# Part of the experts through DRAM, and a new order of the first loads, in a two-layer hybrid decoder

## Chip, cores and metric

The kernel runs on one core of one Trainium2 chip. The metric is the device time of one execution in microseconds (us); lower is better. Shown runs of the kernel before: 1222.70, 1228.84 and 1231.54 us.

## The reference

Two layers, each a mixer and a mixture of experts, over 512 tokens of width 1024, in float32. Both halves are preceded by RMSNorm and modulated by adaLN (shift, scale and gate, from `c_act @ w_ada[l] + b_ada[l]`).

```python
for l in range(DEPTH):
    shift_m, scale_m, gate_m, shift_f, scale_f, gate_f = split(c_act @ w_ada[l] + b_ada[l])
    h = rms_norm(x, norm_mix[l]) * (1 + scale_m) + shift_m
    x = x + gate_m * hybrid_mixer(h, w_in[l], ...)       # stick-breaking + gated linear attention
    h = rms_norm(x, norm_ffn[l]) * (1 + scale_f) + shift_f
    x = x + gate_f * hierarchical_moe(h, ...)
```

The mixture picks one of 4 groups for each token, then 2 of the group's 8 experts, and adds `(silu(h @ w_gate[e]) * (h @ w_up[e])) @ w_down[e]` with the two weights. An expert has 256 hidden units, so its three matrices have 1 MiB each; all 32 experts of a layer are read.

## The kernel before, in words

**Mixer.** `mixer` projects x to all heads in steps of 128 rows of `w_in`: `project` makes a load, a `prep` (split of the weights into a high and a low part) and a `run` of each step, and a list of steps sets their order. In layer 0 the adaLN vectors that the first projection needs are made on the way: `ada` loads 2 tiles of `w_ada`, multiplies them by c (the product `ada`), copies the result (`row`, L245) and turns it into columns (`adaT`). Eight such generators stand in `first`, two for each pair of steps, and all share one PSUM bank. The loads of the first two are issued before anything of `w_in` (L312). `transposed` (L361) runs them to their end before it modulates x. Twelve products of the identity (`warm`) run on TensorE (PE) ahead of that.

**Experts.** `moe` numbers 64 slots for each expert, 2048 in all, and goes over 16 pairs of experts, 128 slots each. The token rows of a pair are fetched from a DRAM copy `xg` by an indirect DMA on GpSimd's queue (`fetch`), transposed (`g`) and modulated (`gT`). Then

- `hidden`: 32 products `gu` with gate and up weights, silu, product: `hs`;
- `turn`: transposition of `hs` (`hsT`) and a copy on ScalarE (`hT`);
- `down`: 16 products `d` with the down weights; DVE scales them by routing weight and gate (`o`), ScalarE and GpSimd split `o` into `ohi` and `olo`;
- `places` and `combine`: a 0/1 matrix `oT` of slots against tokens, and 16 products `y` of `oT` with `ohi` and `olo` that spread the slots' rows to the 512 tokens; DVE adds them to x, one add of 128x512 for each of 8 units.

In the loop over pairs i, PE gets d of pair i-1, gu of pair i, then y of pair i-1 in four parts with transposes of later rows between them, and hsT after the third part.

**What sets the order of the loads.** SP (the sync engine) issues all weights in the order of `queue`: `(0, e)` is gate and up of expert e (5 buffers), `(1, e)` is down (4 buffers). The loop `for i in range(0, NE, 2)` at its head lists them as buffers come free: d of a pair frees two down buffers, gu of a pair two gate and up buffers. An issue waits for its buffer, and all behind it wait too. GpSimd's DMAs have a queue of their own; both run on the same 16 DMA engines.

**What the steps of the prediction touch.** `load_weights` and `queue`, `down`, `places`, the loop over i (from L1247), the head of `mixer` (L306 to L341) and `project`'s `load` and `prep` (L397 to L414).

Of the kernel before, what the change touches and what calls it, by code (L numbers as in the profile page):

```python
# [9 lines left out]
F = mybir.dt.float32  # L10
# [10 lines left out]
P = 128  # L21
# [3 lines left out]
NE, FE, CAP = 32, 256, 64  # L25
NX = 16


@with_exitstack
def hybrid_decoder_kernel(ctx, tc, x, c, w_ada, b_ada, norm_mix, norm_ffn, w_in, w_gk2, b_gk, q_gain,  # L30
# [181 lines left out]
    xs = dram.tile([S, D], F, name="xs")  # L212
    xg = dram.tile([S, D], F, name="xg")

    mod = [const.tile([P, 6, KT], F, name=f"mod{l}") for l in range(L)]
# [4 lines left out]
    bgk = cols[:, 96:100]  # L220


    def ada(l, c0, n, raw, bank, at, later=True):
# [12 lines left out]
        if later and vec in (2, 5) and not half:  # L236
            gates[l, vec] = (gts if vec == 5 else gms[l])([P, D])
            kept_dma(G, gates[l, vec], along(b_ada, l * 6 * D + vec * D, D))
        yield
        row = rowt[at]([P, n], name="row")  # L240

        ps = bank("ada")
        for k in range(KT):
            product(ps[32 * (k % 4):32 * (k % 4) + 32, 0:n], ct1[:, k:k + 1].to_broadcast([P, 32]), ws[k], k < 4, k >= 4)
        A.copy(row, ps[:, 0:n])  # L245
        yield
        if vec in (2, 5):
# [35 lines left out]
    def mixer(l, xt, ss, x_src, pool, later):  # L283
# [21 lines left out]
        if l == 0:  # L305
# [4 lines left out]
            for tt in range(NT):  # L310
                kept_dma(SY, xt[tt // 2][:, tt % 2], x_src[P * tt:P * tt + P, :])
            for g in first[0]:  # L312
                next(g)
        wv = w_in[l].rearrange("(k p) n -> p k n", p=P)
# [3 lines left out]
        for i, g in enumerate((q_gain, k_gain)):  # L318
            for h in range(2):
                G.dma_start(gain[64 * h:64 * h + 64, i:i + 1], g[l].rearrange("(d o) -> d o", o=1))  # L320
        V.tensor_scalar(gain[:, 1:2], gain[:, 1:2], 8.0, None, op0=OP.mult)
        glag = const.tile([P, P], F, name="glag", tag="glag")
# [17 lines left out]
        if l == 0:  # L340
            pm(ps[0:1, 0:1], ss[:, 0, 2:3], ident[:, 0:1], True, True)  # L341
        for _ in range(16 if l else 12):
            pm(ps[:, 0:P], ident, ident, True, True)
# [50 lines left out]
        def project(cols, n, nb, finish, feature=False, lead=False):  # L394
# [3 lines left out]
            def load(k):  # L398
                if k % 2 == 0:
# [5 lines left out]
                    for start, w in cols:  # L405
                        SY.dma_start(t[:, :, at:at + w], wv[:, k:k + 2, start:start + w])
                        at += w
                    held[k], held[k + 1] = t[:, 0], t[:, 1]

            def prep(k):  # L410
                if lead:
                    transposed(k)
                parts[k] = [whl([P, n], R, name="whl") for _ in range(2)]
                split(held.pop(k), *parts[k])  # L414

# [24 lines left out]
        def sb_qk(g):  # L440
            def finish(banks):
                qk = sbq[g] = xq([P, NT, 8, 64], name="qk")
                so = tiny.tile([P, NT, 8], F, name="sqk")
# [419 lines left out]
    def moe(l, xt, ss, pool):  # L863
# [10 lines left out]
        queue = [(0, 0), (0, 1), (0, 2), (0, 3), (0, 4), (1, 0), (1, 1), (1, 2), (1, 3)]  # L874
        for i in range(0, NE, 2):
            queue += [(0, e) for e in (i + 5, i + 6) if e < NE] + [(1, e) for e in (i + 4, i + 5) if e < NE]
        loaded = {}
# [12 lines left out]
        def load_weights(n):  # L890
            for _ in range(min(n, len(queue))):
                w, e = queue.pop(0)
                loaded[w, e] = load_expert(w, lambda src: src[l, e // 8, e % 8])

# [148 lines left out]
        def down(hT, ws, i=None):  # L1043
# [7 lines left out]
            for q in range(2):  # L1051
                pd = bank("d", "dy", 4)
                for j in range(2):
                    for e in range(n):
                        pm(pd[64 * e:64 * e + 64], hT[:, j, 64 * e:64 * e + 64],
                           ws[e][:, D * j + 512 * q:D * j + 512 * q + 512], j == 0, j == 1)
                o = ot([P, 512], name="o")
                gate = gates[l, 5][r, 512 * q:512 * q + 512]
# [3 lines left out]
                else:  # L1062
                    V.scalar_tensor_tensor(o, pd, cws[:, i:i + 1], gate, op0=OP.mult, op1=OP.mult)  # L1063
                    if last is not None:
# [18 lines left out]
        def places(i):  # L1083

            o1 = s2([P, S], name="o1")
            V.tensor_scalar(o1, slots_row[:, 0], sid[:, i:i + 1], None, op0=OP.is_equal)
            oT = (rows_ if i == NE // 2 - 1 else ohs)([P, S], R, name="oT")
            V.scalar_tensor_tensor(oT, slots_row[:, 1], sid[:, i:i + 1], o1, op0=OP.is_equal, op1=OP.add)
            return oT
# [11 lines left out]
        def combine_last(pairs):  # L1101
# [18 lines left out]
            for n, u in ((0, 5), (0, 6), (1, 0), (1, 1), (0, 7), (1, 2), (1, 3), (1, 4), (1, 5), (1, 6), (1, 7)):  # L1120
                unit(n, u)

        def spread(slot, slot0):
# [77 lines left out]
        keep_warm(lo.rearrange("p t e -> p (t e)"), 20)  # L1201
        fetched = [fetch(idx[:, i:i + 1]) for i in range(4)]


        with tc.issue_after(listed.ins), tc.issue_after(normed.ins):
# [15 lines left out]
            V.tensor_tensor(cw[:, :, 1:2], e2, gw, op=OP.mult)  # L1221
            dump(f"cw{l}", cw)
            exw = tmp.rearrange("p t k e -> p (t k) e")
            V.tensor_tensor(exw, ex.rearrange("p t k e -> p (t k) e"), cw.rearrange("p t k -> p (t k)")[:, :, None].to_broadcast([P, NT * 2, NE]), op=OP.mult)
# [20 lines left out]
        gT1, second = gather(fetched[1:2])  # L1245
        hs = None
        for i in range(NE // 2):  # L1247
            while not {(0, 2 * i), (0, 2 * i + 1)} <= set(loaded):
                load_weights(1)
            if i % 2 == 0:  # L1250
                now = gT
                if i < NE // 2 - 2:
                    gT, rest = gather(fetched[i + 2:i + 4])
                    fetched += [fetch(idx[:, j:j + 1]) for j in range(i + 4, min(i + 6, NE // 2))]
# [10 lines left out]
            if i == 0:  # L1265
                for _ in second:
                    pass
                weights_by_slot()
            for u in range(4):
                for v in range(2):  # L1270
                    if i:
                        combine(2 * u + v, *part)
                next(rest, None)
                if u == 2:
                    hT = turn(hs)
        last = []
        end = combine_last([part, last])
# [94 lines left out]
```

## Time and profile before

| | us |
|---|---|
| median of the three runs | 1228.84 |
| lowest, highest | 1222.70, 1231.54 |
| profiled execution | 1228.59 |
| its span, first to last instruction | 1226.4 |
| PE busy in the span | 1174.6 (96%) |
| DVE, ScalarE, GpSimd busy | 686.3, 473.6, 196.7 |
| granted TensorE clock, mean | 0.988 |

The profiled execution is one run; its span leaves out what lies before the first and after the last instruction. A group of rows below names its view. In the chain of waits, each row has a start, a length and what held the end back. In the windows, each row has a stretch and the busy time of each engine in it, the granted clock, the DMA engines' busy share and GB/s. In the rows of one tile, "DMA to landing" is the time from issue to landing of the loads in that window. Matmuls overlap, so a row of PE can be longer than the distance to the next.

### The profile page before, as it was taken

What the parts mean: (1) busy time and instruction counts of PE and PEld (TensorE: products, weight loads), DVE (VectorE), ACT (ScalarE), POOL (GpSimd) and SP (SyncE); (2) the same over time, 40 slices, a digit from 0 to 9 for tenths busy, and PEclk for the clock granted to TensorE, in tenths of its full rate; (3) what the DMA queues carried; (4) which work ended last, traced back from release to release, by engine and by line L of the source; (5) the groups of instructions that cost most, each with busy time, mean ns of one, the idle gap of its engine ahead of it and who ended that gap; (6) DMA issues with size and microseconds to landing.
All of it is one profiled execution on the core that took longest, in us unless ns stands there. A gap on an engine that the chain in (4) does not pass through costs nothing.

```text
span 1226.4 us, 17270 instructions
## 1 busy us (share of the span) xinstructions
PE 1174.6 (96%) x6467; PEld 749.3 (61%) x6467; DVE 686.3 (56%) x1336; ACT 473.6 (39%) x942; POOL 196.7 (16%) x231
## 2 busy tenths in 40 slices
PE   4999999999989999999999997999999899999997
PEld 3787867666765444444478775666876744444443
DVE  3474546465854555555566562545856565555553
ACT  4376656453243111111155764554624411111121
POOL 3000010011312222221110001001210222222110
PEclk8999999999999999999999999999999999999999
DMA  9652765643687999999445355563229599999981
GB/s 297 225 170 88 223 167 148 207 142 101 249 369 263 411 410 417 419 418 419 191 156 173 98 168 121 172 172 121 69 103 372 210 400 420 418 420 419 419 349 69
DMA packets 105926, 312.27 MB, mean 255 GB/s; under 512 B 12876, under 2 KB 49936, under 8 KB 81264
## 3 DMA queue, kind: packets, MB, share of 16 engines
q1 hardware_dynamic: 96720, 289.57, 63.4%
q0 software_dynamic: 9120, 21.57, 5.2%
q8 instruction: 52, 0.85, 0.3%
q14 instruction: 34, 0.28, 0.1%
HBM read 311.08 MB, written 8.40 MB: 260 GB/s over the span
## 4 chain that ended last, share of the span: by engine, by line
PE 85%; DMA 6%; DVE 5%; ACT 2%; issue 1%; SPq 1%; DVEq 0%; ACTq 0%
PE proj L74 19%; PE gu L78 18%; PE y L78 10%; PE d L78 9%; PE op L74 6%; PE z L74 5%; DMA wada<-in_w_ada_dram 3%; PE ada L78 3%; PE g L1003 2%; DMA raw<-in_w_in_dram 2%; PE warm L78 1%; PE pv L74 1%; PE lgT L74 1%; PE o L74 1%; PE adaT L78 1%
## 5 line engine op out<-in xcount | busy, mean ns | idle before, releaser
L78 PE MATMUL gu<-wgu,gT 128*64 128x512 f32 x1024 | 225.4, 592 | 0.1
L74 PE MATMUL proj<-whl,hh 128*128 128x512 f32 (+2 forms) x768 | 218.6, 368 | 0.1
L78 PEld LDWEIGHTS gu<-wgu,gT 128*64 128x64 f32 x1024 | 75.5, 137 | 143.7 <-issue 142.2
L74 PEld LDWEIGHTS proj<-whl,hh 128*128 128x128 f32 x768 | 133.5, 189 | 32.0 <-issue 10.0
L1076 DVE TENSOR_TENSOR x<-y,x 128x512 f32<-128x512 f32 x240 | 148.5, 683 | 0.9 <-PE y L78 0.9
L74 PE MATMUL proj<-whl,hl 128*128 128x512 f32 (+2 forms) x384 | 138.4, 362 | 0.0
L1031 DVE TENSOR_TENSOR hs<-hs,gu 128x256 f32<-128x256 f32 x32 | 13.5, 421 | 198.2 <-ACT hs L1030 198.2
L1069 POOL TENSOR_TENSOR olo<-o,ohi 128x512 fp32r<-128x512 f32 x60 | 76.9, 1283 | 263.5 <-ACT ohi L1068 263.3
L96 DVE TENSOR_TENSOR whl<-raw,whl 128x512 fp32r<-128x512 f32 (+2 forms) x128 | 72.7, 570 | 81.8 <-ACT whl L95 70.5
L78 PE MATMUL d<-wd,hT 128*64 128x512 f32 x512 | 116.9, 598 | 1.4 <-ACT hT L1040 1.4
L78 PE MATMUL y<-ohi,oT 128*128 128x512 f32 x240 | 104.5, 436 | 0.0
L95 ACT ACTIVATE whl<-raw 128x512 fp32r<-128x512 f32 (+2 forms) x128 | 66.6, 524 | 85.1 <-PE proj L74 66.9
L78 PE MATMUL y<-olo,oT 128*128 128x512 f32 x240 | 94.2, 393 | 0.0
L74 PEld LDWEIGHTS proj<-whl,hl 128*128 128x128 f32 x384 | 72.2, 188 | 14.3 <-issue 4.2
L1030 ACT ACTIVATE hs<-gu 128x256 f32<-128x256 f32 x32 | 12.3, 385 | 168.4 <-PE gu L78 168.4
L78 PEld LDWEIGHTS d<-wd,hT 128*64 128x64 f32 x512 | 33.9, 136 | 62.2 <-issue 48.1
L78 PEld LDWEIGHTS y<-ohi,oT 128*128 128x128 f32 x240 | 45.4, 189 | 31.8 <-issue 26.0
L1009 ACT ACTIVATE gT<-g,mod 128x256 f32<-128x256 f32 (+1 forms) x72 | 38.9, 544 | 61.6 <-DVE gT L1011 61.5
L1068 ACT ACTIVATE ohi<-o 128x512 fp32r<-128x512 f32 x60 | 37.8, 630 | 61.6 <-DVE o L1063 61.6
L1063 DVE SCALAR_TENSOR_TENSOR o<-d,cws,gate_f 128x512 f32<-128x512 f32 x64 | 47.8, 750 | 22.7 <-PE d L78 22.7
L736 POOL TENSOR_TENSOR raw<-raw,gate_m 128x1024 f32<-128x1024 f32 x16 | 40.2, 2520 | 122.6 <-DMA raw<-in_w_out_dram 68.2
L78 PE MATMUL ada<-wada,ct 128*32 128x512 f32 x320 | 49.1, 600 | 5.3 <-DMA wada<-in_w_ada_dram 5.3
(346 smaller groups left out, 1951.9 us busy)
## 6 DMA issues: line engine op xcount, KB each, us to landing
wgu<-in_w_gate_dram SPq DMA_DIRECT2D x64, 1024.0 KB, 9.5
wgu<-in_w_up_dram SPq DMA_DIRECT2D x64, 1024.0 KB, 11.7
wd<-in_w_down_dram SPq DMA_DIRECT2D x64, 1024.0 KB, 11.0
wada<-in_w_ada_dram SPq DMA_DIRECT2D x96, 512.0 KB, 5.1
raw<-in_w_in_dram SPq DMA_DIRECT2D x80, 256.0 KB, 4.4
raw<-in_w_out_dram SPq DMA_DIRECT2D x16, 512.0 KB, 4.1
raw<-in_w_in_dram SPq DMA_DIRECT2D x32, 128.0 KB, 4.2
xg<-xn POOLq DMA_DIRECT2D x8, 512.0 KB, 4.9
```

Of the source, the lines that this page charges most:

```text
L74: T.matmul(o, a, b, start=start, stop=stop, skip_group_check=True)
L78: tc.keep_in_program_order(T.matmul(o, a, b, start=start, stop=stop, skip_group_check=True))
L95: A.activation(hi, src, AF.Copy)
L96: eng.tensor_tensor(lo, src, hi.bitcast(F), op=OP.subtract)
L736: G.tensor_tensor(t, t, gates[l, 2][:, None, cols].to_broadcast([P, 2, 512]), op=OP.mult)
L1003: tc.keep_in_program_order(T.transpose(ps[:, at:at + P], r[:, P * k:P * k + P], ident))
L1009: A.activation(o, src, AF.Identity, scale=m, bias=b)
L1031: V.tensor_tensor(hs[r], hs[r], gu[r, 256:512], op=OP.mult)
L1063: V.scalar_tensor_tensor(o, pd, cws[:, i:i + 1], gate, op0=OP.mult, op1=OP.mult)
L1068: A.activation(hi, o, AF.Copy)
L1069: (G if last is None else V).tensor_tensor(lo, o, hi.bitcast(F), op=OP.subtract)
L1076: V.tensor_tensor(xc, ps, xc, op=OP.add)
```

## The change

**Experts.** The pairs are taken in the order of the table `ORDER`, which puts the first four (experts 0 to 7, all of group 0) at positions 1, 4, 7 and 10. For these four, `down` writes the scaled `o` (two tiles of 128x512) to a DRAM tensor `ys` by DMAs on GpSimd's queue; there is no split, no `places` and no `combine`. After the fourth, `take_back` fetches for each of 4 token tiles and 2 choices the 128 rows of `ys` at the tokens' slots (slots past the first 512 are left out by the bounds check), and DVE adds them to x under a mask `ysm`. Six of the eight are issued in steps 12 to 14, two behind the loop. In the step behind a spread pair, `down` comes after `hidden`, and `queue` is listed to match.

**Start.** The first two adaLN generators issue their loads behind those of the first `w_in` tile; the split of that tile's first half stands behind the copy of the adaLN row; `gain` is scaled later; 8 warm-up products in place of 12 in layer 0.

```diff
+NY = 4
+ORDER = [4, 0, 5, 6, 1, 7, 8, 2, 9, 10, 3, 11, 12, 13, 14, 15]
...
-        A.copy(row, ps[:, 0:n])
+        copied.append(A.copy(row, ps[:, 0:n]))
...
-            for g in first[0]:
-                next(g)
...
-        V.tensor_scalar(gain[:, 1:2], gain[:, 1:2], 8.0, None, op0=OP.mult)
...
-        for _ in range(16 if l else 12):
+        for _ in range(16 if l else 8):
...
                     held[k], held[k + 1] = t[:, 0], t[:, 1]
+                    if lead and k == 0:
+                        for g in first.get(0, ()):
+                            next(g)
...
-                split(held.pop(k), *parts[k])
+                if lead and k == 0 and l == 0:
+                    with tc.issue_after(copied[-1].ins):
+                        split(held.pop(k), *parts[k])
+                else:
+                    split(held.pop(k), *parts[k])
...
-        for i in range(0, NE, 2):
-            queue += [(0, e) for e in (i + 5, i + 6) if e < NE] + [(1, e) for e in (i + 4, i + 5) if e < NE]
+
+        freed = [(0, 0)]
+        for i in range(1, NE // 2):
+            freed += [(0, i), (1, i - 1)] if ORDER[i - 1] < NY else [(1, i - 1), (0, i)]
+        for w, i in freed:
+            queue += [(w, e) for e in ((2 * i + 4, 2 * i + 5) if w else (2 * i + 5, 2 * i + 6)) if e < NE]
...
-                o = ot([P, 512], name="o")
+                m = NY if i is None else ORDER[i]
+                o = (ohl if m < NY else ot)([P, 512], name="o")
...
-                    V.scalar_tensor_tensor(o, pd, cws[:, i:i + 1], gate, op0=OP.mult, op1=OP.mult)
+                    V.scalar_tensor_tensor(o, pd, cws[:, m:m + 1], gate, op0=OP.mult, op1=OP.mult)
+                    if m < NY:
+                        kept_dma(G, ys[P * m:P * m + P, 512 * q:512 * q + 512], o)
+                        continue
...
+        def take_back(tt, k):
+
+            r = rows_([P, D], name="back")
+            G.indirect_dma_start(r, None, ys[:, :], bass.IndirectOffsetOnAxis(ap=ysi[:, tt, k:k + 1], axis=0),
+                                 bounds_check=NY * P - 1, oob_is_err=False)
+            xc = xt[tt // 2][:, tt % 2]
+            return lambda: V.scalar_tensor_tensor(xc, r, ysm[:, tt, k:k + 1], xc, op0=OP.mult, op1=OP.add)
...
-            if i:
+            by_dram = i > 0 and ORDER[i - 1] < NY
+            if i and not by_dram:
                 part = places(i - 1), down(hT, [loaded.pop((1, e)) for e in (2 * i - 2, 2 * i - 1)], i - 1)
             *_, hs = hidden(gT1 if i == 1 else now, 0 if i < 2 else P * (i % 2), [loaded.pop((0, e)) for e in (2 * i, 2 * i + 1)])
+            if by_dram:
+                down(hT, [loaded.pop((1, e)) for e in (2 * i - 2, 2 * i - 1)], i - 1)
             load_weights(4)
...
+            if by_dram:
+                for _ in range(4):
+                    next(rest, None)
+                hT = turn(hs)
+                continue
             for u in range(4):
                 for v in range(2):
                     if i:
                         combine(2 * u + v, *part)
+                if i >= NE // 2 - 4 and u % 2 == 0:
+                    taken.append(take_back(*back.pop(0)))
+                    if len(taken) > 1:
+                        taken.pop(0)()
                 next(rest, None)
```

How the order changes, at three places. First SP's list of loads in layer 0's expert stage, behind the nine loads ahead; before, gate and up of two experts and two down loads take turns:

```order
L887 DMA wgu<-in_w_gate_dram 128x2048
L887 DMA wgu<-in_w_up_dram 128x2048
L887 DMA wgu<-in_w_gate_dram 128x2048
L887 DMA wgu<-in_w_up_dram 128x2048
L883 DMA wd<-in_w_down_dram 128x2048 x2
L887 DMA wgu<-in_w_gate_dram 128x2048
L887 DMA wgu<-in_w_up_dram 128x2048
L887 DMA wgu<-in_w_gate_dram 128x2048
L887 DMA wgu<-in_w_up_dram 128x2048
L883 DMA wd<-in_w_down_dram 128x2048 x2
```

and the same list after, from the second step on, where the pair at position 1 is a spread one:

```order
L903 DMA wgu<-in_w_gate_dram 128x2048
L903 DMA wgu<-in_w_up_dram 128x2048
L903 DMA wgu<-in_w_gate_dram 128x2048
L903 DMA wgu<-in_w_up_dram 128x2048
L903 DMA wgu<-in_w_gate_dram 128x2048
L903 DMA wgu<-in_w_up_dram 128x2048
L903 DMA wgu<-in_w_gate_dram 128x2048
L903 DMA wgu<-in_w_up_dram 128x2048
L899 DMA wd<-in_w_down_dram 128x2048 x4
```

Two down loads that stood between the two groups of gate and up now stand behind both, in front of the next two; the same happens behind the spread pairs at positions 4, 7 and 10.

Then PE, from the end of a step on; before, each step has d, gu and the four parts of y:

```order
L1003 MATMUL g<-ident,rows 128x128 x2
L78 MATMUL d<-wd,hT 64x512 x8
L78 MATMUL gu<-wgu,gT 64x512 x16
L78 MATMUL y<-ohi,oT 128x512
L78 MATMUL y<-olo,oT 128x512
L78 MATMUL y<-ohi,oT 128x512
L78 MATMUL y<-olo,oT 128x512
L1003 MATMUL g<-ident,rows 128x128 x2
```

and after, in the step behind a spread pair and the one that follows (a matrix product of float32 is two instructions in the trace and one row here):

```order
L1020 MATMUL g<-ident,rows 128x128 x2
L81 MATMUL gu<-wgu,gT 64x512 x16
L81 MATMUL d<-wd,hT 64x512 x8
L1020 MATMUL g<-ident,rows 128x128 x8
L1055 MATMUL hsT<-ident,hs 128x128 x2
L81 MATMUL d<-wd,hT 64x512 x8
L81 MATMUL gu<-wgu,gT 64x512 x16
L81 MATMUL y<-ohi,oT 128x512
```

The spread pair's d moved behind the next gu, its y are gone, and hsT stands right before the next d.

Last ScalarE at the start of layer 0, where `whl` is the split's high part, `row` the copied adaLN row and `hh` the high part of the modulated x; before:

```order
L353 ACTIVATE x<-x,rs 128x512 x4
L95 ACTIVATE whl<-raw 128x512 x2
L245 COPY row<-ada 128x256 x2
L95 ACTIVATE hh<-hf 128x512
L245 COPY row<-ada 128x256
```

and after:

```order
L356 ACTIVATE x<-x,rs 128x512 x4
L251 COPY row<-ada 128x256 x2
L98 ACTIVATE whl<-raw 128x512 x2
L98 ACTIVATE hh<-hf 128x512
L251 COPY row<-ada 128x256
```

Both copies of a row moved ahead of the two splits of the first `w_in` tile.

## Rows read from the trace of the kernel before

**Rows 1.** The page: span and instructions.
```profile
span 1226.4 us, 17270 instructions
```

**Rows 2.** Windows: stretch; busy PE, PEld, DVE, ACT, POOL; clock; DMA share; GB/s.
```profile
1104.00:1166.00 62.00, 62.00 (x299) 29.43 (x297) 34.48 (x61) 12.35 (x25) 12.19 (x10) 1.00 1.01 419
```

**Rows 3.** Chain of waits, layer 1, one pair: start us, us, what.
```profile
1150.79 3.58 PE d L78 x16
1154.37 6.87 PE gu L78 x32
1161.24 1.12 PE y L78 x4
...
1162.58 0.94 PE y L78 x4
...
1163.73 0.92 PE y L78 x4
...
1165.11 0.92 PE y L78 x4
...
1166.25 3.58 PE d L78 x16
```

**Rows 4.** Loads of wgu from 1145 and from 551; layer 0's chain at d.
```profile
L887 SPq DMA_DIRECT2D wgu<-in_w_up_dram x2: 423/424/424, 1146.2 to 1147.1; - x2
...
DMA to landing us min/median/max: 9.6/12.6/15.7
...
L887 SPq DMA_DIRECT2D wgu<-in_w_up_dram x2: 422/422/423, 552.5 to 553.4; - x2
...
DMA to landing us min/median/max: 8.9/12.0/15.1
...
572.52 3.58 PE d L78 x16
```

**Rows 5.** Tiles wd (issued from 938 to 941) and xg (945).
```profile
L883 SPq DMA_DIRECT2D wd<-in_w_down_dram x3: 328/430/431, 939.1 to 940.0; - x3
...
DMA to landing us min/median/max: 11.0/14.1/16.1
...
L88 POOL DMA_DIRECT2D xg<-xn x1: 595/595/595, 945.4 to 945.4; - x1
```

**Rows 6.** The page's DMA issues: count, KB each, median us to landing.
```profile
out_dram<-x SPq DMA_DIRECT2D x8, 256.0 KB, 2.3
...
rows<-xg,idx POOLq DMA_INDIRECT x32, 8.6
```

**Rows 7.** Timeline of PE at the last pair of layer 1.
```profile
1209.94 3.65 PE L78 MATMUL d<-wd,hT 128*64 128x512 f32 x16 [0.46 <-ACT hT L1040]
```

**Rows 8.** Timeline of PE after two idle times, and the windows behind them.
```profile
765.25 1.11 PE L500 MATMUL qT<-ident,two 128*128 128x128 f32 x4 [6.33 <-ACT w L553]
...
765.00:769.60 4.60, 4.35 (x12) 3.23 (x12) 4.28 (x7) 3.81 (x8) 0.00 (x0) 0.50 0.16 15
...
363.29 0.18 PE L78 MATMUL rk<-both,after_b 128*128 128x32 bf16 x1 [2.16 <-DVE both L951]
...
363.30:366.90 3.60, 3.60 (x28) 3.32 (x29) 2.79 (x10) 0.00 (x0) 0.00 (x0) 0.53 0.40 159
```

**Rows 9.** Chain of waits at the start, and a window in it.
```profile
9.53 11.55 DMA raw<-in_w_in_dram
...
22.62 1.01 PE adaT L74 x4
...
24.37 1.86 PE ada L74 x16
...
16.00:21.00 5.00, 2.28 (x23) 0.95 (x21) 0.94 (x3) 0.00 (x0) 0.00 (x0) 1.00 1.05 362
```

**Rows 10.** Loads of wgu issued from 1176 to 1178.
```profile
L887 SPq DMA_DIRECT2D wgu<-in_w_up_dram x1: 423/423/423, 1177.1 to 1177.1; - x1
...
DMA to landing us min/median/max: 8.5/10.0/11.4
```

More of the change, by code (lines that the diff above doesn't have):

```diff
@@ L213, in hybrid_decoder_kernel @@
     xg = dram.tile([S, D], F, name="xg")
+    ys = dram.tile([NY * P, D], F, name="ys")
     mod = [const.tile([P, 6, KT], F, name=f"mod{l}") for l in range(L)]
@@ L220, in hybrid_decoder_kernel @@
     bgk = cols[:, 96:100]
+    copied = []
     def ada(l, c0, n, raw, bank, at, later=True):
@@ L441, in finish @@
             def finish(banks):
+                if g == 0:
+                    V.tensor_scalar(gain[:, 1:2], gain[:, 1:2], 8.0, None, op0=OP.mult)
                 qk = sbq[g] = xq([P, NT, 8, 64], name="qk")
@@ L892, in load_weights @@
                 w, e = queue.pop(0)
-                loaded[w, e] = load_expert(w, lambda src: src[l, e // 8, e % 8])
+                n = 2 * ORDER[e // 2] + e % 2
+                loaded[w, e] = load_expert(w, lambda src: src[l, n // 8, n % 8])
         load_weights(9)
@@ L1085, in places @@
             o1 = s2([P, S], name="o1")
-            V.tensor_scalar(o1, slots_row[:, 0], sid[:, i:i + 1], None, op0=OP.is_equal)
+            n = ORDER[i]
+            V.tensor_scalar(o1, slots_row[:, 0], sid[:, n:n + 1], None, op0=OP.is_equal)
             oT = (rows_ if i == NE // 2 - 1 else ohs)([P, S], R, name="oT")
-            V.scalar_tensor_tensor(oT, slots_row[:, 1], sid[:, i:i + 1], o1, op0=OP.is_equal, op1=OP.add)
+            V.scalar_tensor_tensor(oT, slots_row[:, 1], sid[:, n:n + 1], o1, op0=OP.is_equal, op1=OP.add)
             return oT
@@ L1121, in combine_last @@
                 unit(n, u)
+        ysi, ysm = pool.tile([P, NT, 2], I32, name="ysi"), t3(2, "ysm")
+        def take_back(tt, k):
[4 more added lines that the diff above has]
+            return lambda: V.scalar_tensor_tensor(xc, r, ysm[:, tt, k:k + 1], xc, op0=OP.mult, op1=OP.add)
         def spread(slot, slot0):
@@ L1201, in moe @@
         keep_warm(lo.rearrange("p t e -> p (t e)"), 20)
-        fetched = [fetch(idx[:, i:i + 1]) for i in range(4)]
+        fetched = [fetch(idx[:, i:i + 1]) for i in ORDER[:4]]
         with tc.issue_after(listed.ins), tc.issue_after(normed.ins):
@@ L1222, in moe @@
             dump(f"cw{l}", cw)
+            V.tensor_scalar(ysi, slot, 65535.0, None, op0=OP.min)
+            V.tensor_scalar(ysm, slot, float(NY * P), None, op0=OP.is_lt)
             exw = tmp.rearrange("p t k e -> p (t k) e")
@@ L1245, in moe @@
         gT1, second = gather(fetched[1:2])
-        hs = None
+        back, taken = [(tt, k) for tt in range(NT) for k in range(2)], []
         for i in range(NE // 2):
@@ L1253, in moe @@
                     gT, rest = gather(fetched[i + 2:i + 4])
-                    fetched += [fetch(idx[:, j:j + 1]) for j in range(i + 4, min(i + 6, NE // 2))]
-            if i:
+                    fetched += [fetch(idx[:, j:j + 1]) for j in ORDER[i + 4:i + 6]]
+            by_dram = i > 0 and ORDER[i - 1] < NY
+            if i and not by_dram:
                 part = places(i - 1), down(hT, [loaded.pop((1, e)) for e in (2 * i - 2, 2 * i - 1)], i - 1)
             *_, hs = hidden(gT1 if i == 1 else now, 0 if i < 2 else P * (i % 2), [loaded.pop((0, e)) for e in (2 * i, 2 * i + 1)])
+            if by_dram:
+                down(hT, [loaded.pop((1, e)) for e in (2 * i - 2, 2 * i - 1)], i - 1)
             load_weights(4)
@@ L1275, in moe @@
                     hT = turn(hs)
+        for tt, k in back:
+            taken.append(take_back(tt, k))
+        for add_back in taken:
+            add_back()
         last = []
```

## The prediction

> **What bounds the kernel now.** I read the page first: a span of 1226.4 us inside a profiled execution of 1228.59 us, so 2.2 us lie around the span [rows 1]. The median of the three runs shown is 1228.84 us; the sum below is made against 1228.59, and the two agree to 0.02%. A measurement of this kernel tells about 1% (12.3 us) from no change.
>
> Then a window of four periods in layer 1's expert stage. PE is busy for the whole 62 us, and so are the DMA engines (share 1.01, 419 GB/s) [rows 2]. The reader is to see that two limits coincide there. Which of them is next when one is loosened decides this case, and busy shares can't tell it.
>
> So I read the chain of waits for one pair of experts [rows 3]: d starts at 1150.79 and again at 1166.25, a period of 15.46 us without a gap: 3.58 for d, 6.87 for gu, four blocks of y (1.12 + 0.94 + 0.92 + 0.92 = 3.90), and transposes. For the other limit: a pair's weights are six transfers of 1 MiB, 6.29 MB, and at 419 GB/s 15.0 us, before the token rows of the pair are fetched. PE never waits for weights today because they land early, not because the stream is quick. How early is read from the loads themselves [rows 4]: in layer 1 the last gate and up of the group issued from 1145.8 were issued at 1147.1 and landed 15.7 us later, at 1162.8; in layer 0 they were issued at 553.4 and landed 15.1 us later, at 568.5.
>
> At the start the reader is to see another chain [rows 9]: the first w_in tile lands at 9.53 + 11.55 = 21.08, ScalarE splits it, only then copies the adaLN row, and PE goes on at 22.62 (adaT) and 24.37 (second ada product, 1.86 us, to 26.23). The DMA engines are full there (share 1.05 from 16 to 21 us).
>
> **What the change takes off PE.** Four of sixteen pairs in each layer lose their y block, 3.90 us each [rows 3]. In those steps hsT stands right before the next d, with nothing between: PE then waits for ScalarE's copy, which today costs 0.46 us in the one place where d follows hsT directly [rows 7]. Saved: 4 x (3.90 - 0.46) = 13.8 us of PE in a layer. That is not yet time, because the next limit is the DMA stream.
>
> **What it adds to the DMA stream.** Each of the four pairs writes two 256 KB tiles: 2.10 MB a layer, 5.0 us at 419 GB/s. The trace has no such write beside the expert stream, so I bound it. Below: nothing, if writes cost the loads no time (7.5 us better over two layers than my sum, worked out under the first rival). Above: a 256 KB store alone takes 2.3 us to land [rows 6], 18.4 us for eight. The nearest row is xg's 512 KB write, issued at 945.4, in the middle of three wd loads [rows 5]. These landed at 939.1 + 11.0 = 950.1, 939.5 + 14.1 = 953.6 and 940.0 + 16.1 = 956.1: 3.5 us apart where 1 MiB at 419 GB/s needs 2.5. So a write costs about its bytes (1.0 us seen, 1.25 by size). I take 5.0 a layer.
>
> **What the new queue order does to it.** This is the step that decides. Behind a spread pair, gu of the next pair now comes ahead of d, and SP's list follows: four gate and up loads stand ahead of the two wd loads that stood ahead of them. The fourth spread pair is tenth from zero. The wd of pair 12 is released by d of pair 10 and now lands when the gate and up behind gu of pair 11 land today, plus the writes: layer 1 at 1162.8 + 5.0 = 1167.8, layer 0 at 568.5 + 5.0 = 573.5. Today d of pair 12 starts at 1166.25 and 572.52 [rows 3, 4]. So it starts 1.6 and 1.0 us later than today, however early PE is: +2.6 us together. The 13.8 us saved before it turn into waits for wd, at the pairs that stand two behind a spread one (6, 9, 12): 13.8 + 1.3, some 15 us a layer, 5 us each. From pair 12 on, nothing of PE's work is left out, so the delay reaches the end. The last gate and up land at 1177.1 + 11.4 = 1188.5 today [rows 10]; their gu comes two periods and a d behind 1166.25, near 1200 by estimate, so 5 us more of writes don't make them late; nor do the take-backs, whose rows are only those of the first eight experts.
>
> **The clock.** After PE idled for 6.33 us the granted clock was 0.50 from 765.0 to 769.6, and after 2.16 us it was 0.53 from 363.3 to 366.9: the lower level, 1.2 GHz [rows 8]. A wait of some 5 us lies between. At half clock some 3.4 us of work lose 1.7 us. Behind the first two waits the loss only shortens the next wait; behind the third it stays: 2 x 1.7 = +3.4 us (bounds 0 and 2.3 a layer, from the same rows). The Trainium skill's page "TensorE: Matmul & The Clock Gate", section "HAM oscillation — how this bites in real kernels", describes this pattern, a kernel that waits for DMA inside its loop and resumes at the low clock; by it the 3.4 stand, without it the sum would be 1227.0.
>
> **Work that I cost at nothing.** DVE is busy for 34.48 of 62 us [rows 2]; a layer loses 32 adds of 128x512 and gains eight of 128x1024, half as many elements. ScalarE and GpSimd lose eight copies and eight subtractions. New waits: the first take-back on GpSimd's queue waits for the fourth pair's writes to land, and behind it stand pair 11's olo; the first take-back's add on DVE waits for a gather (8.6 us to land [rows 6]), and behind it stand two adds of x and a gT. Both lie just ahead of the third wait for wd, where PE idles anyway; without that cover they would cost 2 us or so each.
>
> **The start.** With w_in ahead, the same bytes (cT, x, one w_in tile, four adaLN tiles) cross the same full DMA engines, so the last of them lands near 21.1 whatever the order; now it is the last adaLN tile. The first adaLN row is no longer copied behind the split, and the scaling of gain no longer stands ahead of x's normalization. The second ada product then has its first half done, and ends at 21.1 + 0.9 = 22.0 in place of 26.2: -4.2 us. What follows on PE is in the chain without gaps. Bounds: -5.5, if the next loads gain as well, and -1, if PE runs longer at half clock or the next adaLN tiles land late. Four warm-up products fewer cost nothing: PE waits for adaLN anyway.
>
> **Sum.** 1228.6 - 4.2 + 2.6 + 3.4 = 1230.4; I say 1230.
>
> **Rivals.** First: writes to DRAM cost the loads nothing. Then d of pair 12 is 1166.25 - 1162.8 = 3.45 and 572.52 - 568.5 = 4.0 us early: 1228.6 - 4.2 - 7.5 + 3.4 = 1220.3, or 1216.9 without the clock's loss. For it: loads and writes go opposite ways. Against it: the 3.5 us gap [rows 5]. Second: the stream isn't at its limit, and PE's saving arrives: 1228.6 - 4.2 - 27.6 = 1196.8. For it: PE's gapless chain. Against it: a share of 1.01 and loads that take 9 to 16 us from issue to landing. Third, the slower side: a write from GpSimd's queue costs the weights more than its bytes. At 1.25 us a tile, twice my price, each layer adds 5.0: 1240.4; at 2.3, 8 x 2.3 - 5.0 = 13.4 a layer: 1257. It decides from 1.3 us a tile on. For it: rows of 2 KB, not the weights' 8. Against it: xg's write. The Trainium skill's page "DMA: Bandwidth & Descriptors", section "Anatomy of one DMA — SWDGE (gpsimd) path", fits 2.0 us plus bytes over 436 GB/s for such a DMA; that would be 2.6 us a tile by estimate, if the fixed part held up the weights, and the 3.5 us gap says that it doesn't. Fourth: the start gains nothing, since the later adaLN tiles set the pace there, not this product: 1234.6.
>
> **Chances.** Forecast 0.46, writes free 0.20, PE's saving arrives 0.07, dear writes 0.15, no gain at the start 0.12. Faster by over 1% (below 1216.3) is the second rival and half of the first, whose lower end is 1215.6 with the start's -5.5: 0.17. Slower by over 1% (above 1240.9) is most of the third: 0.12. The rest, 0.71, is within 1%. The range reaches from the first rival's lower end to the cheaper end of the third: 1216 to 1241.
>
> **What would show it.** Right: after, PE waits in both layers for wd by DMA, three times, some 5 us each; d of the thirteenth pair starts 1 to 2 us later from the stage's first gu than today; the DMA share stays at 1.0 through pair 12; the clock falls to 0.5 behind the waits; the second ada product ends near 22 us. Wrong: PE without waits for wd, an expert stage shorter by over 8 us a layer, or weights landing further than 5 us behind today's.

## The result and the profile after

| | before | changed |
|---|---|---|
| median, us (14 runs each) | 1226.10 | 1236.87 |
| lowest to highest | 1221.60 to 1231.54 | 1230.07 to 1239.98 |
| profiled execution | 1228.59 | 1233.80 |
| its span | 1226.4 | 1232.0 |
| PE busy | 1174.6 | 1159.4 |
| DMA moved, MB | 312.27 | 318.89 |

The ratio of the changed kernel to the kernel before is 1.0081, with a 95% interval of 1.0061 to 1.0100: slower by 0.8%, less than the 1% that the prediction counted as a change. The forecast was 1230 us, the range 1216 to 1241; it was summed from 1228.59 us, so its own change was +1.4 us, and the measured one is +10.8. The profiled execution of the kernel before is 2.5 us above the median of its runs, that of the changed one 3.1 us below, so the two traces differ by 5.6 us of span where the medians differ by 10.8. The places of the loss are read from the traces, its size from the runs.

First the windows of the changed kernel, the stretch of [rows 2] and then the third of the three waits for wd (the down weights) in layer 1, at pair 12 (stretch; busy PE, PEld, DVE, ACT, POOL; clock; DMA share; GB/s):

```profile
1104.00:1166.00 62.00, 55.66 (x258) 24.99 (x256) 29.00 (x49) 9.55 (x20) 12.71 (x12) 0.99 1.01 420
1162.00:1173.00 11.00, 8.85 (x26) 2.61 (x28) 4.08 (x7) 1.58 (x3) 2.26 (x2) 0.69 1.02 419
```

PE was busy for 62.00 of 62 us in [rows 2] and is for 55.66 now. The DMA engines moved 419 GB/s and move 420: the stream of weights was full and stays full, and what PE saves turns into waiting. The waits of PE in layer 1's expert stage of the changed kernel say for what (us in total, times, longest):

```profile
PE d L81 <- DMA wd<-in_w_down_dram: 9.4, 6, 3.8
PE d L81 <- ACT hT L1057: 2.8, 6, 0.5
PE y L81 <- POOL olo L1090: 0.7, 1, 0.7
PE y L81 <- DVE x L1097: 0.2, 1, 0.2
```

The 9.4 us stand at the d of pairs 6, 9 and 12, two halves each (one for each expert's wd). Layer 0 waits less:

```profile
PE d L81 <- DMA wd<-in_w_down_dram: 4.0, 4, 1.5
PE d L81 <- DVE oT L1110: 2.3, 1, 2.3
```

The profile puts the 2.3 us, at pair 6, down to `oT`; the wait ended 2.4 us before the second wd of the pair was there, about the distance between the two halves of the other waits (2.4 to 2.6), so the first wd is the likelier cause. The timeline of PE around the first d of the two stages and the waits at pairs 6 and 12 (start, length, count; in brackets the idle time before and what ended it):

```profile
381.29 3.65 PE L81 MATMUL d<-wd,hT 128*64 128x512 f32 x16 [0.24 <-ACT hT L1057]
...
472.63 5.93 PE L81 MATMUL d<-wd,hT 128*64 128x512 f32 x13 [1.35 <-DMA wd<-in_w_down_dram]
...
566.17 1.04 PE L81 MATMUL d<-wd,hT 128*64 128x512 f32 x2 [0.73 <-DMA wd<-in_w_down_dram]
568.75 3.22 PE L81 MATMUL d<-wd,hT 128*64 128x512 f32 x13 [1.53 <-DMA wd<-in_w_down_dram]
...
975.85 3.65 PE L81 MATMUL d<-wd,hT 128*64 128x512 f32 x16 [0.24 <-ACT hT L1057]
...
1068.68 4.87 PE L81 MATMUL d<-wd,hT 128*64 128x512 f32 x13 [0.46 <-DMA wd<-in_w_down_dram]
...
1162.79 1.04 PE L81 MATMUL d<-wd,hT 128*64 128x512 f32 x2 [1.96 <-DMA wd<-in_w_down_dram]
1165.19 6.10 PE L81 MATMUL d<-wd,hT 128*64 128x512 f32 x13 [1.36 <-DMA wd<-in_w_down_dram]
```

A start time by itself compares badly between traces, because the stage begins at another time. So I measure from the stage's first d. In the kernel before, d of pair 12 starts 185.52 us after it in both layers:

```profile
386.93 3.65 PE L78 MATMUL d<-wd,hT 128*64 128x512 f32 x16 [0.24 <-ACT hT L1040]
...
572.45 1.94 PE L78 MATMUL d<-wd,hT 128*64 128x512 f32 x8
...
980.66 3.65 PE L78 MATMUL d<-wd,hT 128*64 128x512 f32 x16 [0.24 <-ACT hT L1040]
...
1166.18 2.37 PE L78 MATMUL d<-wd,hT 128*64 128x512 f32 x10
```

In the changed kernel the second wd of pair 12 is there at 568.75 - 381.29 = 187.46 and at 1165.19 - 975.85 = 189.34: 1.9 and 3.8 us late, where 1.0 and 1.6 were forecast. The d that waited at 1165.19 needs 6.1 us for 13 instructions, at a granted clock of 0.69 in the window above (0.50, the lower of the two levels, 1.2 GHz, from 1164.2 to 1171.0); at 568.75 the same 13 need 3.22.

The account of the 5.6 us of span, from one trace to the other: first d of layer 0's stage 386.93 - 381.29 = 5.6 earlier; layer 0's stage, first d to the end of the last, 235.5 in place of 232.9, +2.6; the second mixer 1.8 shorter, which nothing in the change explains (from last d to first d it took 357.7 to 363.0 us in the traces of this study, all with the same mixer); layer 1's stage 240.3 in place of 232.9, +7.4; from the last d to the program's end 15.8 in place of 12.8, +3.0. The last of these stood in no part of the prediction.

### The profile page after: what moved, and what is told of

Read it like the earlier page. It is cut to its first block, busy times and chain, and to the rows that moved or that the text cites. A ratio compares the mean times of both kernels' runs of the same rounds, so it can differ in the third digit from the quotient of the medians.

```text
span 1232.0 us, 17021 instructions
## 1 busy us (share of the span) xinstructions
PE 1159.4 (94%) x6331; PEld 728.0 (59%) x6331; DVE 666.9 (54%) x1276; ACT 462.5 (38%) x926; POOL 208.0 (17%) x247
## 2 busy tenths in 40 slices
DMA packets 109511, 318.89 MB, mean 259 GB/s; under 512 B 14845, under 2 KB 51905, under 8 KB 84849
## 5 line engine op out<-in xcount | busy, mean ns | idle before, releaser
L81 PE MATMUL gu<-wgu,gT 128*64 128x512 f32 x1024 | 231.4, 593 | 0.1
L81 PE MATMUL d<-wd,hT 128*64 128x512 f32 x512 | 130.9, 629 | 21.5 <-DMA wd<-in_w_down_dram 13.4
L1097 DVE TENSOR_TENSOR x<-y,x 128x512 f32<-128x512 f32 x176 | 109.7, 680 | 3.1 <-PE y L81 3.1
L81 PEld LDWEIGHTS d<-wd,hT 128*64 128x64 f32 x512 | 37.9, 143 | 96.9 <-issue 68.9
L1090 POOL TENSOR_TENSOR olo<-o,ohi 128x512 fp32r<-128x512 f32 x44 | 60.5, 1380 | 133.2 <-ACT ohi L1089 121.0
L81 PE MATMUL y<-ohi,oT 128*128 128x512 f32 x176 | 77.0, 438 | 0.3 <-DVE x L1097 0.3
L1047 ACT ACTIVATE hs<-gu 128x256 f32<-128x256 f32 x32 | 12.3, 384 | 162.5 <-PE gu L81 162.5
L81 PE MATMUL y<-olo,oT 128*128 128x512 f32 x176 | 69.6, 396 | 2.4 <-POOL olo L1090 2.4
L1089 ACT ACTIVATE ohi<-o 128x512 fp32r<-128x512 f32 x44 | 27.7, 630 | 86.7 <-DVE o L1081 83.5
L1057 ACT COPY hT<-hsT 128x256 f32<-128x256 f32 x32 | 11.9, 372 | 111.6 <-PE hsT L1055 111.6
```

The lines of the kernel that those rows point to most:

```text
L81: tc.keep_in_program_order(T.matmul(o, a, b, start=start, stop=stop, skip_group_check=True))
L1089: A.activation(hi, o, AF.Copy)
L1090: (G if last is None else V).tensor_tensor(lo, o, hi.bitcast(F), op=OP.subtract)
L1097: V.tensor_tensor(xc, ps, xc, op=OP.add)
```

## The experiments

My theory: the wd loads that the new order puts behind two groups of gate and up, on a stream that is full, set the time (the order); the writes cost their bytes. The rivals: the writes cost far more than their bytes, or nothing; the start gives nothing; the clock costs nothing. Times from "first d" are those of the stage in question. What a single trace can tell has a limit: in `experts_only`, with the same writes and take-backs, the second wd of pair 12 is there at 189.2 and 189.1 us, so with the 187.5 and 189.3 of the changed kernel this time differs by up to 1.9 us between stages that should be equal.

**The two halves apart.** `start_only` is the kernel before with the hunks of the start; `experts_only` is the changed kernel without them.

> The kernel before with the new start alone. By my theory the start is worth what the changed kernel's trace shows there: the second ada product ends near 21.8 us instead of 26.2, the first d of layer 0's experts starts 5.6 us earlier than 386.93, and since nothing behind it is late the whole program gains 5 to 6 us: ratio near 0.9955. Rival: the early start is lost again in the mixer (late adaLN tiles, a lower clock), then d starts as before and the ratio is 1.000. GpSimd's drain at the end of the program should stay at its 1.94 us, since this kernel adds no transfer on GpSimd's queue.

> The changed kernel with the start of the kernel before. By my theory all of the loss is in the experts and at the program's end: waits of 2 to 4 us for wd at the pairs 6, 9 and 12 of each layer, and a time some 5 us above the changed kernel's, so 15 us above the kernel before: ratio near 1.012. If the new start was itself the cause of lost time, this kernel is not slower than the kernel before by more than 5 us: ratio below 1.005.

Measured: start alone 1223.2 us against 1226.26 before, ratio 0.9979 (0.9960 to 0.9998); experts alone 1240.23 us, ratio 1.0131 (1.0095 to 1.0167). The start gains some 3 us (its interval reaches from 0.2 to 4.9), less than the 5 to 6 expected; its trace has the first d of layer 0's experts 3.8 us earlier than before:

```profile
383.12 3.65 PE L78 MATMUL d<-wd,hT 128*64 128x512 f32 x16 [0.24 <-ACT hT L1048]
```

The same edit in the changed kernel showed 5.6 there. But one execution differs from another by as much: `queue_32_more` (below) has the start of the kernel before, and its first d is 4.8 us earlier than 386.93:

```profile
382.11 3.66 PE L78 MATMUL d<-wd,hT 128*64 128x512 f32 x16 [0.24 <-ACT hT L1044]
```

Over all traces, the first d starts at 382.1 to 386.9 with the old start (three traces) and at 379.6 to 383.1 with the new one (ten), 3.4 us apart in the mean. So no single trace gives the gain, and the 3 us of the runs are the better number. The experts lose 14 us by the medians, 16 by the ratio, and their waits are the same as in the changed kernel (the waits of PE in layer 1's stage of `experts_only`):

```profile
PE d L81 <- DMA wd<-in_w_down_dram: 9.3, 6, 3.6
```

**The order.** `d_first` puts the spread pair's d back ahead of the next gu, and SP's list with it:

```diff
-            freed += [(0, i), (1, i - 1)] if ORDER[i - 1] < NY else [(1, i - 1), (0, i)]
+            freed += [(1, i - 1), (0, i)]
...
-            if i and not by_dram:
+            if by_dram:
+                down(hT, [loaded.pop((1, e)) for e in (2 * i - 2, 2 * i - 1)], i - 1)
+            elif i:
                 part = places(i - 1), down(hT, ...
             *_, hs = hidden(...)
-            if by_dram:
-                down(hT, [loaded.pop((1, e)) for e in (2 * i - 2, 2 * i - 1)], i - 1)
```

> The changed kernel with the down product of a spread pair ahead of the next gate and up product, as everywhere else, and SP's list of loads back in its old order; spread pairs, writes and take-backs stay. By my theory (the place of the wd loads behind two groups of gate and up is what costs): no wait for wd is left; PE gets ahead until the gate and up loads bind. These land 11.2 us before they are needed in the kernel before, the writes take 5.0 of it, so some 6 us a layer are gained; with 5.6 at the start and 3 lost at the program's end the time is some 15 us under the kernel before: ratio near 0.988. Rival (writes from GpSimd's queue cost the stream far more than their bytes, 2 us a tile and more): then the gate and up loads are late too and the ratio stays at 1.005 or above.

Measured: 1217.37 us, ratio 0.9924 (0.9879 to 0.9969). Against the changed kernel's 1.0081 that is 1.6%, 19 us, for the place of one product and two loads, PE's order and SP's list changed together. So the order decides, and dear writes are out. The waits of PE in layer 0's stage, then in layer 1's:

```profile
PE gu L81 <- DMA wgu<-in_w_up_dram: 3.1, 2, 1.8
...
PE d L81 <- DMA wd<-in_w_down_dram: 1.0, 1, 1.0
...
PE gu L81 <- DMA wgu<-in_w_up_dram: 2.6, 2, 2.0
...
PE d L81 <- DMA wd<-in_w_down_dram: 1.0, 1, 1.0
```

PE now runs ahead until gate and up bind. The stages gained 4.0 and 3.0 us, not 6, and one row tells why: in layer 0 the gu of the last pair waited until

```profile
596.80 1.51 PE L81 MATMUL gu<-wgu,gT 128*64 128x512 f32 x6 [1.29 <-DMA wgu<-in_w_up_dram]
```

which is 215.0 us from its first d at 381.79. In the kernel before, the last up was issued at 583.4, landed 10.4 us later, at 593.8, and was needed by the gu at 606.0 (tile wgu, issued from 583 to 584, and the timeline of PE):

```profile
L887 SPq DMA_DIRECT2D wgu<-in_w_up_dram x1: 425/425/425, 583.4 to 583.4; - x1
DMA to landing us min/median/max: 8.3/9.4/10.4
...
605.97 7.04 PE L78 MATMUL gu<-wgu,gT 128*64 128x512 f32 x32
```

That landing is 206.9 us from the first d (593.8 - 386.9). The stream is 8.1 us later by then, not 5.0. The last load was 12.2 us early before, and 12.2 - 8.1 = 4.1 is what PE got in layer 0.

**What the writes cost.** `no_writes` leaves the eight writes of a layer out and lets the take-backs read the token copy `xg`, so that they no longer wait for a write; `writes_twice` issues each write twice, the first time to a second tensor `yt`:

```diff
                     if m < NY:
-                        kept_dma(G, ys[P * m:P * m + P, 512 * q:512 * q + 512], o)
                         continue
...
-            G.indirect_dma_start(r, None, ys[:, :], ...
+            G.indirect_dma_start(r, None, xg[:, :], ...
```
```diff
                     if m < NY:
+                        kept_dma(G, yt[P * m:P * m + P, 512 * q:512 * q + 512], o)
                         kept_dma(G, ys[P * m:P * m + P, 512 * q:512 * q + 512], o)
```

> The changed kernel without the eight writes of scaled rows in each layer (left out: the four spread pairs' results; the take-backs fetch the same number of rows from the token copy instead). By my theory a write costs its bytes, 0.6 us a tile, 5.0 us a layer: the d behind the third wait starts 5 us earlier from the stage's first d in each layer, and the time is 10 us under the changed kernel's, ratio to the kernel before near 1.000. By the rival (a write holds the weights up by 2 us or more) the third wait shrinks by all that PE can gain, and the ratio falls below 0.985. If writes are free, the time stays at the changed kernel's, 1.008.

> The changed kernel with each write of scaled rows issued twice, the first time to a tensor that nobody reads. By the price of no_writes (0.56 us a tile, its bytes at the stream's rate) the second wd of the third wait lands 4.5 to 5 us later from the stage's first d in each layer than in the changed kernel (187.5 and 189.3 us there, so 192 to 194), and the time rises by 10 us, ratio near 1.016. If the first write was cheap because it found room, the second costs more: 10 us a layer. GpSimd's drain at the program's end, 1.94 us with 85 transfers on its queue, 3.16 with 101 and 3.98 with 117, should be near 4.8 us with 133.

Measured: without writes 1222.36 us, ratio 0.9982 (0.9954 to 1.0010); with twice as many 1245.64 us, ratio 1.0146 (1.0084 to 1.0209). The first d and the third wait of both layers in `no_writes`:

```profile
382.12 3.65 PE L81 MATMUL d<-wd,hT 128*64 128x512 f32 x16 [0.24 <-ACT hT L1057]
...
566.20 3.22 PE L81 MATMUL d<-wd,hT 128*64 128x512 f32 x13 [1.35 <-DMA wd<-in_w_down_dram]
...
972.02 3.65 PE L81 MATMUL d<-wd,hT 128*64 128x512 f32 x16 [0.24 <-ACT hT L1057]
...
1155.74 3.22 PE L81 MATMUL d<-wd,hT 128*64 128x512 f32 x13 [1.35 <-DMA wd<-in_w_down_dram]
```

The second wd is there at 184.1 and 183.7 us from the first d, 3.4 and 5.6 earlier than in the changed kernel: 4.5 us for eight tiles in the mean, 0.56 each (4.9 and 0.61 if `experts_only` is averaged in). The ratio falls by 0.0099, 12 us, where 10 were expected. Doubled, the price is cleanest at pair 6, behind four more tiles. In `writes_twice`:

```profile
474.91 4.75 PE L81 MATMUL d<-wd,hT 128*64 128x512 f32 x13 [1.36 <-DMA wd<-in_w_down_dram]
...
1077.43 5.56 PE L81 MATMUL d<-wd,hT 128*64 128x512 f32 x13 [0.78 <-DMA wd<-in_w_down_dram]
```

With its first d at 380.69 and 982.36, that is 94.2 and 95.1 us, against 91.3 and 92.8 in the changed kernel: 2.6 us for four tiles, 0.64 each. Both are 256 KB at some 419 GB/s (0.63). At pair 12 the expectation can't be read, because PE reached that d after the weights: the take-back waited longer, and `olo` behind it held up y by 3.5 and 1.7 us in layer 0. The time rose by 8 us by the ratios, with two runs, where 10 were expected.

**What the take-backs cost.** `no_take_back` leaves the take-backs and their adds out and keeps the writes.

```diff
-                    taken.append(take_back(*back.pop(0)))
...
-        for tt, k in back:
-            taken.append(take_back(tt, k))
```

> The changed kernel without the eight take-backs and their adds in each layer (left out: the spread pairs' results never reach x); the writes stay. If the take-backs that are issued ahead of the third wait for wd delay it, its second wd lands about 2 us earlier from the stage's first d (187.5 and 189.3 us in the changed kernel); if they don't, it lands as there. GpSimd's drain should be 3.16 us with 101 transfers. Time: 4 to 7 us under the changed kernel's, ratio near 1.004.

Measured: 1229.44 us, ratio 1.0059 (1.0032 to 1.0086). The third wait's second wd is there 186.3 and 188.5 us from the first d (567.58 - 381.27 and 1162.39 - 973.87), 1.1 and 0.8 earlier:

```profile
567.58 3.22 PE L81 MATMUL d<-wd,hT 128*64 128x512 f32 x13 [1.35 <-DMA wd<-in_w_down_dram]
...
1162.39 4.92 PE L81 MATMUL d<-wd,hT 128*64 128x512 f32 x13 [1.36 <-DMA wd<-in_w_down_dram]
```

That is half of the 2 us expected, and within the 1.9 us by which equal stages differ, so the delay by the take-backs is likely and not clear. The time is 2.7 us under the changed kernel's by the ratios, whose intervals overlap; 4 to 7 were expected. One more thing is gone: from d of pair 12 to d of pair 13 the changed kernel needs 12.5 us from end to start, the kernel before 11.8 (1169.83 to 1181.64), this one 11.8 again. The timeline of DVE in the changed kernel shows what stands there:

```profile
1179.04 0.42 DVE L1048 TENSOR_TENSOR hs<-hs,gu 128x256 f32<-128x256 f32 x1 [6.46 <-ACT hs L1047]
1179.38 1.88 DVE L1097 TENSOR_TENSOR x<-y,x 128x512 f32<-128x512 f32 x3
1181.18 1.27 DVE L1153 SCALAR_TENSOR_TENSOR x<-back,ysm,x 128x1024 f32<-128x1024 f32 x1
1182.37 0.68 DVE L1097 TENSOR_TENSOR x<-y,x 128x512 f32<-128x512 f32 x1
1182.97 0.53 DVE L1028 TENSOR_SCALAR gT<-g,mod 128x256 f32<-128x256 f32 x1
```

The add of a take-back (1.27 us) stands between the adds that free PE's banks, in a step in which PE has nothing to wait for otherwise: 0.7 us a layer, gone with the take-backs.

**The clock.** `warm_in_wait` is the changed kernel with work for PE inside the waits:

```diff
+            if i > 2 and not by_dram and ORDER[i - 3] < NY:
+                keep_warm(ident, 10)
             if i and not by_dram:
```

> The changed kernel with ten products of the identity ahead of the d that waits behind each spread pair, 2.2 us of PE at full clock, shorter than the waits. By the theory that idle time of PE lowers the granted clock, the clock stays at 1.0 from 1155 to 1173 us (0.69 in the changed kernel from 1162 to 1173), the d behind the third wait ends 3.7 us after its second wd landed in both layers (3.6 and 6.5 in the changed kernel), and the time falls by 0 to 3.4 us: ratio 1.005 to 1.008. By the rival, that the clock falls there whatever PE does, or that the loss is hidden, nothing changes; if the products themselves delay d, the ratio is 1.010 or more.

Measured: 1230.32 us, ratio 1.0043 (1.0011 to 1.0075); against the changed kernel 0.4%, some 4.6 us. The windows of its third wait, layer 0 and layer 1:

```profile
555.00:575.00 20.00, 18.86 (x98) 9.74 (x96) 10.14 (x16) 3.05 (x6) 7.92 (x7) 1.00 1.02 418
1162.00:1173.00 11.00, 9.28 (x44) 3.10 (x44) 3.38 (x6) 1.82 (x3) 2.89 (x3) 1.00 1.02 420
```

The clock stays at 1.00 (2.4 GHz, the upper level) where layer 1 had 0.69, and the 13 products of d behind the wait take 3.22 us in both layers (6.10 in layer 1 of the changed kernel). So work in the waits keeps the clock up: that the idle time lowers it is shown. What it is worth in time is not. The intervals of the two ratios overlap a little, and in the traces the two expert stages together are no shorter (237.3 + 238.7 us from first d to the end of the last, against 235.5 + 240.3): the second wd came at 189.2 and 190.5 us from the first d, later than in the changed kernel.

**Fewer spread pairs.** `d_first` with two and with three spread pairs, at positions 4 and 8, and 3, 6 and 9 (`NY` and `ORDER` alone):

> As d_first, but two spread pairs a layer instead of four, at positions 4 and 8. By my theory (the gate and up loads land 11.2 us ahead of need in the kernel before, and writes and take-backs eat that) the writes cost 2.5 and the take-backs some 1.5 us a layer, 7.2 us are left, and PE's saving of 2 x 3.44 = 6.9 us a layer arrives in full: no wait for weights, time from the stage's first d to the last 6.9 us shorter than before in both layers, total -13.8 - 4 at the start + 2.6 at the program's end = -15 us, ratio near 0.988. Rival (the take-backs cost the same however few rows they bring, since there are eight either way): PE waits for gate and up at the last pairs and the ratio stays near 0.992, as in d_first.

> As d_first, but three spread pairs a layer, at positions 3, 6 and 9. By my theory writes and take-backs take some 3.75 + 2.2 of the 11.2 us, so 5.2 of the 10.3 us saved on PE arrive in each layer: total -10.4 - 4 + 2.8 = -11.6 us, ratio near 0.9905, between two and four pairs. If PE's work were still the limit, three pairs would beat two: 0.984.

> The kernel of d_first_ny3 once more, in more rounds, since it is the best so far with two runs only: by both looks at it the ratio lies between 0.983 and 0.995, so it should be 0.989 and the upper end of its interval below 0.995.

Measured: two pairs 1215.54 us, ratio 0.9898 (0.9852 to 0.9943); three pairs 1214.1 us, 0.9890 (0.9829 to 0.9950), and in more runs 1211.22 us, 0.9909 (0.9887 to 0.9931). All beat both kernels; between two, three and four pairs these runs can't choose. With two pairs no wait for weights is left, as expected, but each stage gained 4.9 us and not 6.9 (228.1 from first d to the end of the last, 232.9 before): a step with a spread pair takes 12.5 us in place of 15.46, so it saves 2.95 and not 3.44, and the 0.7 us of the take-back's add goes off.

**GpSimd's drain.** The rows of the program's last line showed a difference that I had not looked for, and `queue_32_more` is the kernel before with 32 small loads more on GpSimd's queue:

```diff
+            spare = const.tile([P, 32], F, name="spare", tag="spare")
+            A.copy(spare, xn[3][:, 512:544])
+            for j in range(32):
+                G.dma_start(spare[0:64, j:j + 1], q_gain[l].rearrange("(d o) -> d o", o=1))
```

> The kernel before with 32 loads of 256 bytes added to GpSimd's queue early in the second mixer, where GpSimd has little to do; nobody reads them. If GpSimd's drain at the end of the program grows with the number of transfers that its queue has carried, whatever they are, it takes 3.9 to 4.0 us here (117 transfers, as in the changed kernel) instead of 1.94, and the program is about 2 us longer: ratio 1.001 to 1.003. If it is the writes or the indirect transfers that the drain waits for, it stays at 1.94 us and the ratio at 1.000.

Measured: 1225.83 us against 1222.74 before, ratio 1.0024 (1.0000 to 1.0048); its drain took 2.84 us, where 3.9 to 4.0 or 1.94 were expected. What that shows stands in the last section.

## Why the prediction was right or wrong

**What bounds the kernel: right.** The DMA share stays at 1.01, PE's share falls, and `d_first` (gate and up bind), `no_writes` and `writes_twice` all move with the stream and not with PE's work. The second rival (PE's saving arrives) falls with it: PE's work is 15.2 us less in the span and the program is longer.

**Writes cost their bytes: right.** 5.0 us a layer were forecast; taking the writes away gave 4.5 in the mean of two layers (3.4 and 5.6), doubling them 0.64 a tile, 5.1 for eight. So the first rival (free) and the third (dear) both fall. The Trainium skill's page "DMA: Bandwidth & Descriptors", section "Anatomy of one DMA — SWDGE (gpsimd) path", has 2.0 us of fixed cost in such a DMA; the runs show that this part isn't taken from the loads beside it.

**The new order delays wd: right in place, short in size.** The waits came where they were forecast, at pairs 6, 9 and 12, in both layers. They were not 5 us each: 9.4 us in layer 1 and 6.3 in layer 0 (with the 2.3 put down to `oT`) in place of 15, since part of what PE saved went into the lower clock behind pair 6 (13 instructions of d in 5.93 and 4.87 us in place of 3.22) and, in layer 0, into a wait of 1.7 us for `olo`. At pair 12 the delay was 1.9 and 3.8 us, forecast 1.0 and 1.6. The term that was short is the landing of wd, "when the gate and up behind gu of pair 11 land today, plus the writes": it has nothing for the take-backs, which the prediction weighs for the last gate and up alone. Two take-backs are issued ahead of the last wait and a third within it, and without the take-backs the weights come 1.1 and 0.8 us earlier, about as much as two equal stages differ. The other 1.4 us of layer 1 are open; the same wait fell at 189.2 and 189.1 in `experts_only`, so the two layers don't differ by nature. In `d_first` the last load was 8.1 us late where the writes explain 5.

**The clock: right in sum, by chance.** 1.7 us in each layer were forecast; the trace has none in layer 0 and 6.10 - 3.22 = 2.9 in layer 1, beyond the upper bound of 2.3. `warm_in_wait` shows that the idle time is the cause, as the Trainium skill's page "TensorE: Matmul & The Clock Gate", section "HAM oscillation — how this bites in real kernels", has it; the clock of 0.69 and 1.00 in the two windows agrees. Whether a wait lowers the clock differed from wait to wait: 1.96 + 1.36 us idle lowered it in layer 1, 0.73 + 1.53 in layer 0 did not.

**Work costed at nothing: half wrong.** I named the take-back's add on DVE and the take-back on GpSimd's queue, and took the third wait for their cover. For GpSimd that held; the timeline of POOL in the changed kernel:

```profile
1143.68 0.58 POOL L91 DMA_DIRECT2D ys<-o  x1 [1.09 <-DVE o L1081]
1151.51 1.06 POOL L1150 DMA_INDIRECT back<-ys,ysi  x1 [7.25 <-DMA ys<-o]
1152.59 1.29 POOL L1090 TENSOR_TENSOR olo<-o,ohi 128x512 fp32r<-128x512 f32 x1
1154.05 1.03 POOL L1150 DMA_INDIRECT back<-ys,ysi  x1 [0.17 <-PE gu L81]
```

The take-back waits 7.25 us for the writes to land, `olo` behind it is late, and PE loses 0.7 us to it (1.7 in layer 0) just ahead of a longer wait for wd. The next take-back's add, one step on, has no cover: 0.7 us a layer, 1.3 in all.

**The start: right in place, some 3 us of the 4.2.** The second ada product was to end near 22.0; it does at 20.73 + 1.08 = 21.8:

```profile
20.73 1.08 PE L77 MATMUL ada<-wada,ct 128*32 128x256 f32 x8 [1.61 <-DMA wada<-in_w_ada_dram]
```

-4.2 us were forecast for that product, and it ends 4.4 us earlier. Of this some 3 us reach the program by the runs of the start alone; the -5.6 and -3.8 of the two traces are no better than the 4.8 us by which two traces of the old start differ. The fourth rival (no gain) is unlikely, but the interval of the start alone ends just below no change, at 0.9998.

**The program's end: missing in the sum.** +3.0 us in the trace, 2.0 of it GpSimd's drain. No term of the sum looked at what the change leaves behind on a queue.

Together: the stages were forecast at +6.0 and came to +10.0 (landing +3.1, clock -0.5, adds +1.3), the end at 0 and came to +3.0, the start at -4.2 and came to -3 to -5.6. The forecast of less than 1% held, and the direction was that of the sum, but there was luck in it: the sum was +1.4 us and the measured change +10.8, short by the terms that it left out, and 1% is 12.3. One of the chances doesn't follow either: half of the first rival was counted as faster by over 1% (below 1216.3), though its sums were 1220.3 and 1216.9.

## What to carry to other kernels

Where PE and the DMA stream are both full, the most that less work on PE can give is how early the weights land, less what the change itself adds to the stream: read landing against need at the last tile first. Moving a product behind another one moves the release of its buffer too, and with it its next load behind a whole group of others; here that turned a gain of some 9 us into a loss of 11. Two or three pairs taken off PE gave as much as four, as far as these runs can tell: with two no wait for weights was left, with four PE waited for gate and up.

## What the runs showed that was not expected

The program's last line waits for GpSimd to drain, and that took longer in these runs the more its DMA queue had carried. The rows of that line (count; min, median, max in ns), with the number of transfers that GpSimd issued in the program; the kernel before (85 transfers):

```profile
L1368 POOLq DRAIN  x3: 51/103/1937, 1223.7 to 1226.2; - x3
```

the changed kernel (117: 16 writes and 16 take-backs more):

```profile
L1418 POOLq DRAIN  x3: 51/103/3978, 1227.2 to 1231.7; - x3
```

`no_writes` and then `no_take_back` (101 each):

```profile
L1417 POOLq DRAIN  x3: 51/103/3162, 1215.0 to 1218.7; - x3
```
```profile
L1415 POOLq DRAIN  x3: 51/103/3162, 1222.7 to 1226.4; - x3
```

`writes_twice` (133; near 4.8 us were expected), and `queue_32_more` (117, the 32 more with 64 rows each, the others with 128):

```profile
L1420 POOLq DRAIN  x3: 51/103/5367, 1235.9 to 1241.8; - x3
```
```profile
L1372 POOLq DRAIN  x3: 51/103/2835, 1217.9 to 1221.3; - x3
```

Writes and take-backs count alike, and 32 small loads made 600 us before the end lengthen it too, so it is not a wait for late data. That it goes by the number of transfers alone is out: 117 gave 3.98 and 2.84. The 32 loads have as many rows as 16 transfers of 128, which cost 1.22 where these cost 0.90; whether rows are the measure was not tried further. What the drain costs the whole program the times can't settle: 0.9 us lies within the interval of `queue_32_more` (0 to 5.9 us). Besides the drain, the kernels with four spread pairs have 0.9 to 1.1 us more between the last d and the drain's start; the traces don't name its cause.
